# Widening the stretch of retention in which no adaLN sums are placed

## The chip, the cores and the metric

The kernel runs on one core of one Trainium2 chip. The metric is the device time of one execution in microseconds. Three executions of the kernel before are at hand, and one more that was profiled.

## What is computed

A decoder trunk of two layers over 256 tokens of 1024 features. Each layer is a half-step SwiGLU FFN, a mixer (retention in layer 0, a gated short convolution in layer 1) and a second half-step FFN. Every sub-layer works on an RMS norm that is scaled, shifted and gated by numbers which a conditioning vector gives (adaLN). Cut to what matters here:

```python
mod = (silu(c) @ ada_w[l] + ada_b[l])            # 9 x 1024 numbers a layer: shift, scale, gate of 3 sub-layers
h = rmsnorm(x, norm_g) * (1 + scale) + shift      # each sub-layer's input
x = x + gate * sublayer(h)                        # 0.5 * gate in the two FFNs

proj = h @ w_in                                   # retention: q, k, v of 4 heads, and g
o = rmsnorm((q k^T * decay) v, gn_g)              # per head, 256 queries, 512 value features
y = (silu(g) * o) @ w_out
```

## The kernel before

The 256 tokens lie along the free axis, features along the 128 partitions. Each float32 operand is split into a high and a low half in float32r, and a product is three products of halves (`product`, L278). A weight tile of 1 MB (128 x 2048) goes through the same stations every time: a DMA on SyncE's queue into one of five raw buffers (L235), a cast to the high half on ScalarE (`split_high`, L248, two pieces of 1024 columns), the low half by a subtraction on VectorE or, for every third tile's second piece, on GpSimd (L253), then TensorE. The list `jobs` (L200 to L223) holds all weight tiles in their order, and `weights()` (L268) hands out the next one and prepares the tiles up to four ahead. One gate tile or output tile of 1 MB takes TensorE about 5.6 us.

Retention (L634) runs its tiles in this order: three gate tiles, eight query and key tiles, eight value tiles (two for each of heads 0 to 3), the other five gate tiles, eight output tiles. From the first value tile on, a list of steps (L734 to L744) interleaves four things: the value projection of a head or a gate tile; `values` of the head before (L694: scores times values on TensorE, two copies out of PSUM on ScalarE at L705, four squares at L344, three additions of squares on GpSimd at L351); `normalize` of the head before that (L713: a sum over partitions on TensorE at L361, a square root on ScalarE at L373, a reciprocal on VectorE at L379, four multiplications at L717); and `apply` (L725: the normalized head times silu(g) at L729, split into halves `og` at L334 and L335). A gate tile leaves PSUM through a copy on ScalarE (L315) and an addition on VectorE (L316), and ScalarE then takes its silu in two halves (L321). Silu and square root need different tables on ScalarE, and a scheduler puts an ACT_TABLE_LOAD wherever the next function's table is not the one loaded. Of PSUM's four buffers one holds the conditioning vector by then, so the products turn over in three.

The conditioning product runs beside all that, off TensorE. `ada_load` (L109) fetches a 1 MB tile of `ada_w` into a raw buffer, and `ada_reduce` (L116) makes two sums of it on VectorE (one multiply-and-sum of 1024 columns and one read of the accumulator each, L120). 64 such tiles are placed among the weight tiles by `pace` (L187), which `weights()` calls for every tile n from the ninth on: it first makes the sums of tiles that were loaded, and then loads the next one if the count of loaded tiles is behind a straight line over the blocks of weights. It does neither around the first tile of an output product (`outputs`), nor for the first three tiles of a sub-layer (`begins`, `BIASED` = 3). Whatever a sub-layer still lacks is forced by `need` (L182), for the scale at the sixth output block and for the gate ahead of the outputs. A scheduler then orders each engine's instructions by readiness and priority; engines run what they hold in that order.

The next sub-layer's input is made as the output blocks are finished: `residual` (L510: L516, L518, L521 or L523), a square (L344), and `scaled` (L395), which makes h = x * scale in halves (L414 on ScalarE, L415 on VectorE) and therefore needs the scale. `whole` (L434) later makes the normalized input from the reciprocal r (L440, L441, L334, L335).

Of the kernel before, what the change touches and what calls it, by code (L numbers as in the profile page):

```python
# [31 lines left out]
BIASED = 3  # L32
# [3 lines left out]
BEFORE = 1  # L36
BEHIND = 1
# [29 lines left out]
def trunk_kernel(ctx: ExitStack, tc: tile.TileContext, a: dict, out: bass.AP):  # L67
# [97 lines left out]
    @within(behind)  # L165
    def reduce_loaded():
        while loaded:
            loaded.pop(0)()

    @within(behind)  # L170
    def run_side():
        kind, *args = side.pop(0)
        if kind == "ada":
            raw = ada_load(*args)
            loaded.append(lambda: ada_reduce(*args, raw))
            state["ada"] += 1
        elif kind == "table":
            nc.sync.dma_start(out=table, in_=a["table"])
        else:
            loaded.append(lambda: (ada_scale if kind == "scale" else ada_gate)(*args))  # L180
# [6 lines left out]
    def pace(n):  # L187

        state["spent"] += jobs[n][1] // P
        if any(o - BEFORE <= n < o + BEHIND for o in outputs) or any(b <= n < b + BIASED for b in begins):
            return
        reduce_loaded()
        if side and state["ada"] < n_ada * state["spent"] / (PACE * n_blocks):
            run_side()


    jobs = []  # L200
    outputs = []
    begins = []
    ready = {}
    for l in range(DEPTH):
        for f in range(2):
            if f == 1:
                begins.append(len(jobs))
                if l % 2 == 0:
                    jobs += [(a["ret_g"][j], 2048) for j in range(BIASED)]
                    jobs += [(a["ret_qk"][j], 2048) for j in range(8)]  # L210
                    jobs += [(a["ret_v"][h, i], 2048) for h in range(HEADS) for i in range(2)]
                    jobs += [(a["ret_g"][j], 2048) for j in range(BIASED, 8)]
                    outputs.append(len(jobs))
                    jobs += [(a["ret_out"][d], 2048) for d in range(KB)]
                else:
                    jobs += [(a["conv_cu"][d], 2048) for d in range(KB)]
                    jobs += [(a["conv_b"][j], 2048) for j in range(KB // 2)]
                    outputs.append(len(jobs))
                    jobs += [(a["conv_out"][j], 2048) for j in range(KB // 2)]
            begins.append(len(jobs))  # L220
            jobs += [(a["ffn_in"][l, f, b], 2048) for b in range(FB)]
            outputs.append(len(jobs))
            jobs += [(a["ffn_out"][l, f, d, i], 1408) for d, i in OUT_ORDER]  # L223
# [44 lines left out]
    def weights():  # L268
        n = state["next"]
        state["next"] += 1  # L270
        while state["loaded"] < min(n + AHEAD, len(jobs)):
            prepare_next()
        if n >= FIRST_GROUP:
            pace(n)
        return ready.pop(n)
# [618 lines left out]
```

## Time and profile before

| what | value |
|---|---|
| three executions | 1076.92, 1080.54 and 1081.19 us, median 1080.54 |
| the profiled execution | 1079.4 us |
| its span | 1077.6 us |
| TensorE, matmul busy | 1051.5 us, 98% of the span |
| VectorE, ScalarE, GpSimd busy | 845.5, 622.0 and 410.7 us |
| DMA | 268.39 MB, mean 249 GB/s |
| mean granted TensorE clock | 0.996 of full speed |

The span is what the profiler saw of the program on the core; 1.8 us of the execution's own time lie around it. Busy shares are means over stages; where an engine idles and what ended the idle time tells which of them sets the end.

### The profile page before, as it was taken

The numbers are of one execution on the slowest core, as the hardware profiler recorded it, in microseconds if no ns is written. First come the engines' busy times: TensorE is split into PE (matmuls) and PEld (weight loads), VectorE is DVE, ScalarE is ACT, GpSimd is POOL, SyncE is SP. The second block draws the span as 40 slices with busy tenths as digits, with TensorE's granted clock in tenths as the row PEclk, the third lists the DMA queues.
The fourth block names the chain that finished last, engine by engine and source line by source line (L and its number), as shares of the span: only waits on it lengthen the run. The fifth ranks groups of instructions, "written<-read, shape, count | busy, mean of one in ns | idle before, by whom it ended". The sixth has DMA issues, their size and how long they took to land.

```text
span 1077.6 us, 17508 instructions
## 1 busy us (share of the span) xinstructions
PE 1051.5 (98%) x6642; PEld 945.9 (88%) x6642; DVE 845.5 (78%) x1137; ACT 622.0 (58%) x1048; POOL 410.7 (38%) x357
## 2 busy tenths in 40 slices
PE   8999999999998999999999999999999989999996
PEld 6999988999886889888888988888898889888885
DVE  6899777899658898997777899777799888655444
ACT  4365545763366667566555766655576577655442
POOL 1034356254335432433345243335433433324352
PEclk9999999999999999999999999999999999999999
DMA  9977788868565576787679778777877544554441
GB/s 340 368 277 275 296 279 314 314 224 326 225 234 196 195 290 221 289 325 280 241 234 323 262 294 319 272 253 265 311 254 261 207 161 175 199 201 139 148 134 40
DMA packets 44566, 268.39 MB, mean 249 GB/s; under 512 B 4801, under 2 KB 6977, under 8 KB 19906
## 3 DMA queue, kind: packets, MB, share of 16 engines
q1 hardware_dynamic: 43138, 266.56, 68.1%
q8 instruction: 52, 0.85, 0.3%
q10 hardware_dynamic: 1344, 0.71, 0.2%
q14 instruction: 32, 0.26, 0.1%
HBM read 266.20 MB, written 1.05 MB: 248 GB/s over the span
## 4 chain that ended last, share of the span: by engine, by line
PE 57%; DVE 3%; issue 1%; ACT 0%; DVEq 0%; ACTq 0%
PE ps L288 33%; PE ps L292 19%; PE ps L291 2%; PE ps L290 2%; DVE lo L253 1%; DVE whole L335 0%; DVE rsum L518 0%; PE ps L361 0%; DVE h L415 0%; DVE raw L816 0%; ACT hi L248 0%; DVE xr L440 0%; DVE r L812 0%; DVE sum L328 0%; DVE av L594 0%
## 5 line engine op out<-in xcount | busy, mean ns | idle before, releaser
L253 DVE TENSOR_TENSOR lo<-raw,hi 128x1024 fp32r<-128x1024 f32 (+1 forms) x300 | 370.4, 1244 | 148.9 <-ACT hi L248 138.1
L248 ACT CAST hi<-raw 128x1024 fp32r<-128x1024 f32 (+2 forms) x408 | 377.0, 937 | 167.0 <-PE ps L288 65.5
L288 PE MATMUL ps<-whole,hi 128*128 128x512 f32 x1136 | 398.8, 396 | 2.4 <-ACT std L373 1.6
L292 PE MATMUL ps<-whole,lo 128*128 128x256 f32 x1264 | 353.8, 280 | 0.0
L253 POOL TENSOR_TENSOR lo<-raw,hi 128x384 fp32r<-128x384 f32 (+1 forms) x108 | 202.6, 1877 | 230.0 <-ACT hi L248 228.4
L288 PEld LDWEIGHTS ps<-whole,hi 128*128 128x128 f32 x1136 | 213.7, 188 | 53.3 <-ACT std L373 2.0
L292 PEld LDWEIGHTS ps<-whole,lo 128*128 128x128 f32 x1264 | 239.4, 189 | 0.1
L288 PE MATMUL ps<-act,hi 128*128 128x512 f32 x616 | 217.7, 398 | 0.6 <-DVE rsum L518 0.6
L292 PE MATMUL ps<-act,lo 128*128 128x256 f32 x704 | 197.8, 281 | 0.0
L335 POOL TENSOR_TENSOR act<-av,act 128x256 fp32r<-128x256 f32 x88 | 81.9, 933 | 202.4 <-ACT act L334 201.6
L120 DVE CUSTOM_DVE_ANT_0 raw<-raw,ps,misc 128x1024 f32<-128x1024 f32 x124 | 154.7, 1274 | 0.0
L288 PEld LDWEIGHTS ps<-act,hi 128*128 128x128 f32 x616 | 115.7, 188 | 29.7 <-DVE rsum L518 1.6
L292 PEld LDWEIGHTS ps<-act,lo 128*128 128x128 f32 x704 | 133.1, 189 | 0.3 <-DVE lo L253 0.3
L290 PE MATMUL ps<-h,hi 128*128 128x258 f32 (+1 forms) x464 | 131.8, 284 | 1.0 <-DVE sum L328 0.9
L291 PE MATMUL ps<-h,hi 128*128 128x258 f32 (+1 forms) x464 | 131.0, 282 | 1.5 <-DVE h L415 1.4
L292 PE MATMUL ps<-h,lo 128*128 128x258 f32 (+1 forms) x464 | 130.3, 281 | 0.0
L291 PEld LDWEIGHTS ps<-h,hi 128*128 128x128 f32 x464 | 87.9, 190 | 2.5 <-DVE h L415 2.4
L290 PEld LDWEIGHTS ps<-h,hi 128*128 128x128 f32 x464 | 87.6, 189 | 1.5 <-ACT sg L321 1.1
L292 PEld LDWEIGHTS ps<-h,lo 128*128 128x128 f32 x464 | 87.6, 189 | 0.0
L334 ACT CAST act<-av 128x256 fp32r<-128x256 f32 x88 | 35.3, 405 | 77.0 <-DVE av L592 70.5
L316 DVE TENSOR_TENSOR sum<-ps,sum 128x512 f32<-128x512 f32 x71 | 48.7, 685 | 19.7 <-ACT sum L315 19.7
L321 ACT ACTIVATE sg<-sum 128x256 f32<-128x256 f32 x79 | 32.6, 415 | 47.7 <-DVE sum L316 25.7
(135 smaller groups left out, 1425.4 us busy)
## 6 DMA issues: line engine op xcount, KB each, us to landing
raw<-in_ffn_in SPq DMA_DIRECT2D x80, 1024.0 KB, 4.9
raw<-in_ada_w SPq DMA_DIRECT2D x64, 1024.0 KB, 5.1
raw<-in_ffn_out SPq DMA_DIRECT2D x64, 704.0 KB, 5.1
raw<-in_ada_w SPq DMA_DIRECT2D x16, 512.0 KB, 7.2
raw<-in_ffn_in SPq DMA_DIRECT2D x16, 512.0 KB, 8.2
raw<-in_ret_g SPq DMA_DIRECT2D x8, 1024.0 KB, 4.9
raw<-in_ret_qk SPq DMA_DIRECT2D x8, 1024.0 KB, 5.3
raw<-in_ret_v SPq DMA_DIRECT2D x8, 1024.0 KB, 5.0
```

What stands on the lines that cost most here:

```text
L120: ins = nc.vector.tensor_tensor_reduce(out=w, in0=w, in1=state["cond"], scale=1.0, scalar=misc[:, C_ADAB + 72 * l + col:C_ADAB + 72 * l + ...
L248: nc.scalar.copy(out=hi, in_=raw[:, c:c + m])
L253: eng.tensor_tensor(out=lo, in0=raw, in1=hi, op=ALU.subtract)
L288: nc.tensor.matmul(out=ps, lhsT=hi, rhs=m.rearrange("p n s -> p (n s)"), start=start, stop=False)
L290: nc.tensor.matmul(out=ps, lhsT=hi, rhs=m[:, 0], start=start, stop=False)
L291: nc.tensor.matmul(out=ps, lhsT=hi, rhs=m[:, 1], start=False, stop=False)
L292: nc.tensor.matmul(out=ps[:, :n], lhsT=lo, rhs=m[:, 0], start=False, stop=stop)
L316: nc.vector.tensor_tensor(out=y[:, :, :S], in0=ps[:, :, :S], in1=y[:, :, :S], op=ALU.add)
L321: nc.scalar.activation(out=out, in_=y[:, i, :S], func=AF.Silu)
L334: hi = nc.scalar.copy(out=dst[:, 0], in_=src)
L335: lo = eng.tensor_tensor(out=dst[:, 1], in0=src, in1=dst[:, 0].bitcast(F32), op=ALU.subtract)
```

## The change

`pace` gets a length for every start in `begins`. The starts that were there keep three tiles. One more is added: from the last value tile on (`len(jobs) - 1` at that point of the list), six tiles, which are this value tile and the five gate tiles behind it. The last gate tile was already left out before, being next to the first output tile.

```diff
         state["spent"] += jobs[n][1] // P
-        if any(o - BEFORE <= n < o + BEHIND for o in outputs) or any(b <= n < b + BIASED for b in begins):
+        if any(o - BEFORE <= n < o + BEHIND for o in outputs) or any(b <= n < b + m for b, m in begins):
             return
@@
             if f == 1:
-                begins.append(len(jobs))
+                begins.append((len(jobs), BIASED))
                 if l % 2 == 0:
                     jobs += [(a["ret_g"][j], 2048) for j in range(BIASED)]
                     jobs += [(a["ret_qk"][j], 2048) for j in range(8)]
                     jobs += [(a["ret_v"][h, i], 2048) for h in range(HEADS) for i in range(2)]
+                    begins.append((len(jobs) - 1, 9 - BIASED))
                     jobs += [(a["ret_g"][j], 2048) for j in range(BIASED, 8)]
                     outputs.append(len(jobs))
@@
-            begins.append(len(jobs))
+            begins.append((len(jobs), BIASED))
             jobs += [(a["ffn_in"][l, f, b], 2048) for b in range(FB)]
```

The changed file has one blank line more above L193 and one line more in the list, so its lines below are numbered two higher (L323 there is L321 here). Since a scheduler orders the instructions, three places are shown in the built programs' order, before and after.

First, ScalarE from the copy of the first gate tile behind the values (`sum`) to the squares of head 3 (`sq<-o`), before:

```order
L315 COPY sum<-ps 128x2x256
L373 ACTIVATE std<-ps,eps 128x256
L334 CAST h_4447<-mod_95 128x2
L321 ACT_TABLE_LOAD
L321 ACTIVATE gate<-sum 128x256 x2
L705 COPY o<-ps 128x512 x2
L344 ACTIVATE sq<-o 128x256 x3
```

and with the change:

```order
L317 COPY sum<-ps 128x2x256
L323 ACT_TABLE_LOAD
L323 ACTIVATE gate<-sum 128x256
L375 ACT_TABLE_LOAD
L375 ACTIVATE std<-ps,eps 128x256
L323 ACT_TABLE_LOAD
L323 ACTIVATE gate<-sum 128x256
L707 COPY o<-ps 128x512 x2
L346 ACTIVATE sq<-o 128x256 x3
```

The square root `std` of head 2 now stands between the two silu halves, with a table load on either side of it, and the cast of a shift (`h<-mod`) is gone from here.

Second, VectorE at the same place, from the low half of a gate tile's weights on, before:

```order
L253 TENSOR_TENSOR lo<-raw,hi 128x1024
L120 ISA raw,mod_95<-raw,ps,misc 128x1024
L120 ISA mod_95 128x1
L120 ISA raw,mod_95<-raw,ps,misc 128x1024
L120 ISA mod_95 128x1
L316 TENSOR_TENSOR sum<-ps,sum 128x2x256
L379 RECIPROCAL r<-std 128x256
L717 SCALAR_TENSOR_TENSOR o<-o,misc,r 128x256 x4
L729 TENSOR_TENSOR o<-o,gate 128x256 x2
```

and with the change:

```order
L255 TENSOR_TENSOR lo<-raw,hi 128x1024
L318 TENSOR_TENSOR sum<-ps,sum 128x2x256
L731 TENSOR_TENSOR o<-o,gate 128x256
L381 RECIPROCAL r<-std 128x256
L731 TENSOR_TENSOR o<-o,gate 128x256
L719 SCALAR_TENSOR_TENSOR o<-o,misc,r 128x256 x4
```

The two sums of an adaLN tile (L120) are gone, and the two products of head 1 with the gate tile moved to both sides of the reciprocal.

Third, VectorE at the entry of the FFN behind retention, from the last output block's residual (`x_94<-ps`) to the reciprocal r of the new norm, before:

```order
L523 SCALAR_TENSOR_TENSOR x_94<-ps,gt_104,x_94 128x256
L351 TENSOR_TENSOR acc<-acc,sq 128x256
L415 SCALAR_TENSOR_TENSOR h_4519<-x_94,sc_99,h_4519 128x256
L253 TENSOR_TENSOR lo<-raw,hi 128x1024
L379 RECIPROCAL r<-std 128x256
```

and with the change:

```order
L525 SCALAR_TENSOR_TENSOR x_94<-ps,gt_104,x_94 128x256
L255 TENSOR_TENSOR lo<-raw,hi 128x1024
L353 TENSOR_TENSOR acc<-acc,sq 128x256
L417 SCALAR_TENSOR_TENSOR h_4514<-x_94,sc_99,h_4514 128x256
L120 ISA raw,mod_95<-raw,ps,misc 128x1024
L120 ISA mod_95 128x1
L120 ISA raw,mod_95<-raw,ps,misc 128x1024
L120 ISA mod_95 128x1
L255 TENSOR_TENSOR lo<-raw,hi 128x1024
L381 RECIPROCAL r<-std 128x256
```

One adaLN tile's sums now stand between the last half of h and the reciprocal. TensorE's own order is the same in both programs.

## Rows read from the trace of the kernel before

**Rows 1.** The profile page: the span, the engines' busy time with share and instruction count.

```profile
span 1077.6 us, 17508 instructions
PE 1051.5 (98%) x6642; PEld 945.9 (88%) x6642; DVE 845.5 (78%) x1137; ACT 622.0 (58%) x1048; POOL 410.7 (38%) x357
```

**Rows 2.** What TensorE waited for over the whole span: the waiting line and what released it, us in total, times, the longest.

```profile
PE ps L361 <- POOL acc L351: 3.4, 1, 3.4
...
PE ps L288 <- ACT std L373: 1.6, 1, 1.6
PE ps L291 <- DVE h L415: 1.4, 2, 0.8
...
PE ps L288 <- DVE whole L335: 0.8, 1, 0.8
```

**Rows 3.** TensorE in order of time around its longest wait: start, us, instruction, and in brackets the idle time before it with what released it.

```profile
338.42 0.50 PE L288 MATMUL ps<-whole,hi 128*128 128x512 f32 x1 [1.60 <-ACT std L373]
...
344.06 0.28 PE L292 MATMUL ps<-whole,lo 128*128 128x256 f32 x1
347.70 0.70 PE L361 MATMUL ps<-acc,ones 128*128 128x256 f32 x2 [3.36 <-POOL acc L351]
```

**Rows 4.** The stretch right behind that wait and the next one: us, busy time of each engine, the granted TensorE clock as a share of full speed, DMA share, GB/s.

```profile
348.70:352.10 3.40, 3.40 (x12) 2.87 (x11) 3.14 (x4) 1.68 (x3) 0.62 (x1) 0.50 0.01 2
352.10:365.00 12.90, 12.90 (x76) 11.27 (x75) 9.77 (x15) 9.54 (x15) 4.30 (x5) 1.00 0.52 186
```

**Rows 5.** ScalarE in order of time from the gate tile's copy to the table load for head 3's square root.

```profile
337.42 0.58 ACT L315 COPY sum<-ps 128x512 f32<-128x512 f32 x1
337.89 0.47 ACT L373 ACTIVATE std<-ps,eps 128x256 f32<-128x256 f32 x1
340.29 0.20 ACT L334 CAST h<-mod 128x2 fp32r<-128x2 f32 x1 [1.92 <-DVE mod L120]
340.50 1.28 ACT L321 ACT_TABLE_LOAD   x1
341.80 0.72 ACT L321 ACTIVATE gate<-sum 128x256 f32<-128x256 f32 x2
342.43 1.05 ACT L705 COPY o<-ps 128x512 f32<-128x512 f32 x2
343.37 1.04 ACT L344 ACTIVATE sq<-o 128x256 f32<-128x256 f32 x3
...
346.13 1.04 ACT L248 CAST hi<-raw 128x1024 fp32r<-128x1024 f32 x1
347.19 1.28 ACT L373 ACT_TABLE_LOAD   x1
```

**Rows 6.** VectorE in order of time at the same place.

```profile
337.78 1.27 DVE L120 CUSTOM_DVE_ANT_0 raw<-raw,ps,misc 128x1024 f32<-128x1024 f32 x1
...
340.18 0.68 DVE L316 TENSOR_TENSOR sum<-ps,sum 128x512 f32<-128x512 f32 x1
340.78 1.73 DVE L379 RECIPROCAL r<-std 128x256 f32<-128x256 f32 x1
342.55 1.68 DVE L717 SCALAR_TENSOR_TENSOR o<-o,misc,r 128x256 f32<-128x256 f32 x4
```

**Rows 7.** GpSimd in order of time at the same place.

```profile
344.29 0.10 POOL L378 MEMSET r<- 128x2 f32 x1 [3.54 <-DVE o L717]
344.38 1.10 POOL L351 TENSOR_TENSOR acc<-sq 128x256 f32<-128x256 f32 x1
345.56 0.72 POOL L351 TENSOR_TENSOR acc<-acc,sq 128x256 f32<-128x256 f32 x1
346.24 0.73 POOL L335 TENSOR_TENSOR og<-o,og 128x256 fp32r<-128x256 f32 x1
346.92 0.72 POOL L351 TENSOR_TENSOR acc<-acc,sq 128x256 f32<-128x256 f32 x1
347.60 1.72 POOL L335 TENSOR_TENSOR og<-o,og 128x256 fp32r<-128x256 f32 x1
```

**Rows 8.** VectorE, and one instruction of GpSimd, in order of time at the entry of the FFN behind retention.

```profile
411.52 0.41 DVE L351 TENSOR_TENSOR acc<-acc,sq 128x256 f32<-128x256 f32 x1
...
413.83 2.39 POOL L253 TENSOR_TENSOR lo<-raw,hi 128x1024 fp32r<-128x1024 f32 x1 [6.72 <-ACT hi L248]
414.10 2.40 DVE L351 TENSOR_TENSOR acc<-acc,sq 128x256 f32<-128x256 f32 x1 [1.38 <-ACT sq L344]
416.43 0.47 DVE L415 SCALAR_TENSOR_TENSOR h<-x,sc,h 128x256 fp32r<-128x256 f32 x1
418.45 1.23 DVE L253 TENSOR_TENSOR lo<-raw,hi 128x1024 fp32r<-128x1024 f32 x1 [1.56 <-ACT hi L248]
419.60 1.75 DVE L379 RECIPROCAL r<-std 128x256 f32<-128x256 f32 x1
```

**Rows 9.** TensorE's two waits in that FFN's first tiles, in order of time.

```profile
416.95 0.39 PE L291 MATMUL ps<-h,hi 128*128 128x258 f32 x1 [0.59 <-DVE h L415]
...
434.79 0.50 PE L288 MATMUL ps<-whole,hi 128*128 128x512 f32 x1 [0.80 <-DVE whole L335]
```

**Rows 10.** Two tiles of that FFN with an adaLN tile beside each: columns as in rows 4 (TensorE, its weight loads, VectorE, ScalarE, GpSimd).

```profile
446.80:452.40 5.60, 5.60 (x34) 4.85 (x33) 5.60 (x7) 3.04 (x6) 4.58 (x3) 1.00 1.00 383
452.40:458.00 5.60, 5.60 (x34) 4.86 (x33) 5.60 (x9) 3.29 (x6) 1.11 (x3) 1.00 1.01 405
```

## The prediction

> **What bounds the kernel now.** I read the profile page first: TensorE's matmuls are busy for 1051.5 of 1077.6 us [rows 1], so no engine beside it can give more than TensorE's own idle time, some 26 us in the whole program. The list of what TensorE waited for comes next. Its longest single wait is 3.4 us for an addition on GpSimd, and the next one inside the program's body is 1.6 us for a square root on ScalarE [rows 2]. TensorE in order of time puts both into the stretch that the change touches: the gate tile that starts at 338.42 came 1.60 us late, and behind it the sum of head 3's squares at 347.70 came 3.36 us late [rows 3]. The reader is to see a third loss there: right behind the long wait the granted clock is 0.50, TensorE's 1.2 GHz, for 3.40 us, and 1.00, or 2.4 GHz, afterwards [rows 4]. At half the rate 3.40 us do 1.70 us of work, so the fall cost 1.70 us. Together 1.60 + 3.36 + 1.70 = 6.66 us hang on this place, and that is the most that can be won here.
>
> Why was it late? Follow ScalarE and VectorE through it. VectorE was free of the tile's low half at 337.78, made two sums of an adaLN tile (1.20 us from start to start and a second one like it), and came to the gate tile's addition only at 340.18 [rows 6]. ScalarE waited 1.92 us for the second of these sums with the cast of a shift, loaded the silu table at 340.50, ran two silu halves, and only at 342.43 copied head 3 out of PSUM; the squares began at 343.37 [rows 5]. GpSimd added them from 344.38 to 347.64, with a product for `og` between the additions [rows 7], and TensorE went on at 347.70. So an adaLN tile did stand in the chain. The question is what stands there when it is gone.
>
> **Step 1: head 3's squares.** Removed: two sums, 340.18 - 337.78 = 2.40 us on VectorE, and ScalarE's wait for them. The gate tile's copy starts at 337.42 for 0.58 us as before, as nothing ahead of it moves, so ScalarE is free at 338.00, and not at 340.50: 2.50 us earlier. Added, as the order shows: the silu table, one silu half, the square root's table, the square root of head 2, the silu table again, the other half. A table load is 1.28 us, with 0.02 us to its activation (340.50 to 341.80), a silu half 0.36 us (half of 0.72), the root 0.47 us [rows 5]. From 338.00: load until 339.28, half until 339.66, load until 340.96, root until 341.45, load until 342.75, half until 343.13. Head 3's copies then start at about 343.10 in place of 342.43. The root was free before, since it ran inside the 1.92 us wait; now it and two more loads are in the path: 2 x 1.30 + 0.47 + 0.10 = 3.17 us put in for 2.50 us taken out, a net delay of 0.67 us.
>
> GpSimd gives most of this back. Before, its first addition had to wait for a memset that waited for VectorE until 344.29, although the second square was done at about 344.10, and took 1.10 us where the others take 0.72 [rows 7]. With the change that memset comes after two additions. The second square ends at 344.10 + 0.67 = 344.77; additions until 345.55 and 346.27, the memset 0.10, `og` 0.73, the last addition 0.72: 347.82, against 347.64 before. The memset needs the four multiplications of head 2: root until 341.45, reciprocal 1.73 (343.18), one gate product about 0.40, multiplications 1.68, so 345.3; that is in time. **Step 1: +0.18 us.** Lower end: had the two added loads cost nothing, -2.60 + 0.18 = -2.4 us. Upper end: the first addition at 1.10 again (+0.38) and the `og` at 1.72, as the next one took [rows 7] (+0.99): +1.6 us. I take +0.18, from the durations met most often.
>
> TensorE's wait ahead of it changes its name, not its worth. The gate tile took its PSUM buffer behind head 2's root; now it takes the one that the former gate tile's addition frees, which can run at 338.05 (copy done) for 0.68 us, so TensorE starts at about 338.75, not 338.42 [rows 3, 5, 6]. These 0.33 us lie in front of a wait that ends by GpSimd anyway: 0.
>
> **Step 2: the clock.** TensorE would still idle from 338.75 + 5.92 (338.42 to 344.34, when it went idle) = 344.67 to 347.85, 3.2 us against 3.36. The nearest row is the wait of 3.36 us, after which the clock fell [rows 3, 4]; I take the fall as unchanged, 0. Ends: -1.70 without it, +1.70 with a second one elsewhere.
>
> **Step 3: the second adaLN tile of the stretch.** It leaves VectorE between the fifth and the seventh gate tile. TensorE waited for nothing there, and ran at full clock [rows 4]: 0.
>
> **Step 4: where the tiles go.** Two tiles are owed. They follow one per weight tile in the output blocks, so the scale of the next sub-layer comes later, and the h halves of blocks 0 to 3 are made in one group. The count of sums ahead of the last h is the same. But one tile's two sums now stand between that h and the reciprocal r. Before, VectorE idled 1.56 us there for a cast [rows 8]. Of 2.40 us, 1.56 are hidden and 0.85 us are not: r at 420.45, not 419.60. All of `whole` hangs on r, VectorE has no gap behind it, and TensorE waited 0.80 us for its seventh part [rows 9]; that wait becomes 1.65. **Step 4: +0.85 us.** Lower end: the last h comes earlier, since its addition took 2.40 us beside a GpSimd subtraction [rows 8] where the one at 411.52 took 0.41; then TensorE's 0.59 us at 416.95 [rows 9] go, and less of the 0.85 is left: -0.6. Upper end: nothing is hidden, +2.4.
>
> **Step 5: the catching up.** Up to eight FFN tiles in a row then carry an adaLN tile, where there were five. Such a tile already fills VectorE (5.60 of 5.60 us) and the DMA engines (share 1.00), yet TensorE stays busy for all of it [rows 10]. What lags by a tile or two is caught by PSUM's three buffers and the weights prepared four tiles ahead: 0. Upper end: one lost overlap like the 2.00 us too long addition of rows 8, +2.0.
>
> **The sum** is +0.18 + 0.85 = +1.0 us on the profiled execution's 1079.4: 1080.4 us. The median of the runs shown is 1.1 us higher, 1080.54, and would give 1081.5; I forecast between the two, **1080.9 us**, no change that can be told from none. About 0.5% (5.4 us) is what a measurement of this kernel can resolve.
>
> The Trainium skill speaks against this change: "ScalarE: Activation LUTs", section "What ACT_TABLE_LOAD costs", puts a drain of some 1.38 us on top of each load, 2.66 us in all. The row does not agree: a cast that began at 346.13 for 1.04 us is followed by a load at 347.19, 0.02 us after it ended [rows 5]. By the page's figure step 1 would cost 2.8 us more, an estimate.
>
> **The rivals.**
>
> *A, the intended gain (0.06).* The chain ends as much earlier as the sums were long: the wait of 3.36 us shrinks by 2.4, and the clock does not fall: -2.4 - 1.7 = -4.1, with step 4 at its lower end -4.7: 1074.7 us. For it: the sums stood in the chain [rows 5, 6]. Against it: two table loads take their place, and every load in these rows takes 1.28 us. Only the whole 6.66 us would pass 0.5%.
>
> *B, a slower one (0.07), at the FFN's entry.* VectorE's two sums ahead of r fall on the same time as a GpSimd subtraction, and r and `whole` pay for both: 2.40 for the sums, 2.0 for an operation held up as at 414.10 [rows 8], and TensorE's wait of then 0.80 + 4.4 = 5.2 us is followed by a fall of the clock as behind the 3.36 us one, 1.70: +6.1 plus step 1, 1085.7 us. It decides from the point where r is more than about 2.5 us late, at 422. Against it: VectorE's idle 1.56 us are there to be filled.
>
> *C, the loads cost double (0.03).* If each switch also emptied the engine for about as long again, step 1 would be 2 x 1.3 = 2.6 us worse: 1083.5 us. The skill's figure above would make it so; the row at 347.19 stands against it.
>
> *D, it does not do what it says.* Only one of the two tiles that leave stood in head 3's chain, and the tile whose sums run ahead of head 1's root stays, being loaded before the last value tile. That is part of the forecast.
>
> **The numbers.** The forecast's case has 0.84: its own ends are 1076.0 (runs as scattered as before, 1076.92 the lowest, with the clock's fall gone) and 1085.5 (1081.19, the highest, with steps 1 and 4 at their upper ends, 1.4 + 1.6 more, and some of step 5). This already reaches C, and A and B lie just outside: range 1076.0 to 1085.5. Faster by over 0.5% needs the most of A: 0.03. Slower by over 0.5% is B with a little of step 5: 0.05. Within: 0.92.
>
> **What would show it.** ScalarE's rows would show three table loads between the gate tile's copy and head 3's copies, and these copies about 5.7 us behind the copy's start (343.10 - 337.42; 5.01 before). TensorE's longest wait would still be for the addition on GpSimd, at 3.0 to 3.7 us, with one stretch at a granted clock of 0.50 behind it; its wait at the gate tile would name VectorE. At the FFN's entry an L120 pair would stand ahead of the reciprocal, and the wait for `whole` would be about 1.6 us. The prediction is wrong if the long wait falls below 1.5 us, if the low clock is gone or comes twice, or if TensorE idles in the eight FFN tiles.

## The result, and the profile after

The changed kernel takes 1082.26 us (median of 20 runs, 1078.63 to 1085.48), the kernel before 1079.94 us (20 runs, 1076.2 to 1083.27): a ratio of 1.0020 with a 95% interval of 1.0011 to 1.0029, so 1.2 to 3.1 us slower, 2.2 in the middle. That is less than the 0.5% named as the limit, but with 20 runs of each kernel it can be told from none, and it is about a microsecond more than the sum in the prediction. The profiled execution took 1081.45 us. Of the runs further below, one execution of copies_first_b, 1144.89 us, was in a slower state of the chip and counts in no ratio and no mean clock.

The page of the changed kernel, for [rows 1]: a longer span, with all engines' work the same to within 3 us.

```profile
span 1079.7 us, 17502 instructions
PE 1054.0 (98%) x6642; PEld 948.2 (88%) x6642; DVE 846.2 (78%) x1137; ACT 624.4 (58%) x1050; POOL 413.2 (38%) x357
```

TensorE in order of time, for [rows 2, 3, 9], and the stretches of low clock with one of full clock, for [rows 4] (columns as there).

```profile
339.55 0.50 PE L290 MATMUL ps<-whole,hi 128*128 128x512 f32 x1 [2.02 <-DVE sum L318]
...
348.85 0.70 PE L363 MATMUL ps<-acc,ones 128*128 128x256 f32 x2 [1.90 <-POOL acc L353]
...
417.81 0.36 PE L293 MATMUL ps<-h,hi 128*128 128x258 f32 x1 [1.88 <-DVE h L417]
...
436.33 0.50 PE L290 MATMUL ps<-whole,hi 128*128 128x512 f32 x1
```

```profile
340.16:343.56 3.40, 3.40 (x13) 2.81 (x12) 1.92 (x2) 3.34 (x5) 0.63 (x1) 0.50 0.52 149
348.85:352.25 3.40, 3.40 (x19) 3.00 (x20) 3.18 (x3) 2.63 (x5) 1.62 (x1) 1.00 0.01 2
418.68:422.08 3.40, 3.40 (x16) 3.25 (x16) 3.40 (x6) 3.23 (x4) 0.00 (x0) 0.50 0.85 328
```

Three things moved. The wait for the gate tile grew from 1.60 to 2.02 us. The low clock came 8.5 us earlier, inside that tile: TensorE worked more slowly on a tile behind which it had to wait anyway, so the wait for head 3's squares reads 1.90 instead of 3.36, and the stretch behind it runs at full clock. From the gate tile's first matmul to the sum of squares it is 348.85 - 339.55 = 9.30 us, and 9.28 before [rows 3]. And the FFN's entry has a wait of 1.88 us for h where there was one of 0.59, with a second stretch of low clock behind it. The matmul that waited 0.80 us for `whole` before, the one at 436.33 here, waits no more; but it stands 18.52 us behind the one that waited for h, where it stood 434.79 - 416.95 = 17.84 behind it [rows 9].

ScalarE and GpSimd at head 3, for [rows 5, 7], from the gate tile's copy on.

```profile
338.13 0.57 ACT L317 COPY sum<-ps 128x512 f32<-128x512 f32 x1
338.72 1.28 ACT L323 ACT_TABLE_LOAD   x1
340.01 0.42 ACT L323 ACTIVATE gate<-sum 128x256 f32<-128x256 f32 x1
340.45 1.28 ACT L375 ACT_TABLE_LOAD   x1
341.74 0.47 ACT L375 ACTIVATE std<-ps,eps 128x256 f32<-128x256 f32 x1
342.23 1.28 ACT L323 ACT_TABLE_LOAD   x1
343.53 0.42 ACT L323 ACTIVATE gate<-sum 128x256 f32<-128x256 f32 x1
343.85 1.06 ACT L707 COPY o<-ps 128x512 f32<-128x512 f32 x2
...
345.67 0.91 POOL L353 TENSOR_TENSOR acc<-sq 128x256 f32<-128x256 f32 x1 [4.88 <-ACT sq L346]
346.66 0.73 POOL L353 TENSOR_TENSOR acc<-acc,sq 128x256 f32<-128x256 f32 x1
...
348.07 0.72 POOL L353 TENSOR_TENSOR acc<-acc,sq 128x256 f32<-128x256 f32 x1
```

The three table loads stand there. Head 3's copies start 343.85 - 338.13 = 5.72 us behind the gate tile's copy (5.01 before), and the last addition ends 348.79 - 338.13 = 10.66 us behind it (347.64 - 337.42 = 10.22 before): 0.44 us late.

VectorE at the FFN's entry with one instruction of GpSimd, for [rows 8].

```profile
405.50 1.27 DVE L120 CUSTOM_DVE_ANT_0 raw<-raw,ps,misc 128x1024 f32<-128x1024 f32 x1
...
406.70 1.27 DVE L120 CUSTOM_DVE_ANT_0 raw<-raw,ps,misc 128x1024 f32<-128x1024 f32 x1
...
412.09 1.21 DVE L255 TENSOR_TENSOR lo<-raw,hi 128x1024 fp32r<-128x1024 f32 x1
413.62 1.20 DVE L255 TENSOR_TENSOR lo<-raw,hi 128x1024 fp32r<-128x1024 f32 x1
413.75 3.64 POOL L255 TENSOR_TENSOR lo<-raw,hi 128x1024 fp32r<-128x1024 f32 x1 [6.78 <-ACT hi L250]
414.76 0.41 DVE L353 TENSOR_TENSOR acc<-acc,sq 128x256 f32<-128x256 f32 x1
415.09 2.58 DVE L417 SCALAR_TENSOR_TENSOR h<-x,sc,h 128x256 fp32r<-128x256 f32 x1
...
421.13 1.74 DVE L381 RECIPROCAL r<-std 128x256 f32<-128x256 f32 x1
```

Two adaLN tiles' sums now follow each other (403.96 to 409.10), since the owed tiles came late and `need`, called at the sixth output block, also makes the sums of the tile just loaded. They push two low halves of weights to 412.09 and 413.62, onto the start of GpSimd's subtraction, which takes 3.64 us in place of 2.39. The addition that took 2.40 us before takes 0.41, but h itself takes 2.58 in place of 0.47 and ends when the subtraction does.

### The profile page after: what moved, and what is told of

Same layout as the page of the kernel before. It is cut to its first block, busy times and chain, and to the rows that moved or that the text cites. A ratio compares the mean times of both kernels' runs of the same rounds, so it can differ in the third digit from the quotient of the medians.

```text
span 1079.7 us, 17502 instructions
## 1 busy us (share of the span) xinstructions
PE 1054.0 (98%) x6642; PEld 948.2 (88%) x6642; DVE 846.2 (78%) x1137; ACT 624.4 (58%) x1050; POOL 413.2 (38%) x357
## 4 chain that ended last, share of the span: by engine, by line
PE 59%; DVE 2%; issue 0%; ACT 0%; DVEq 0%; ACTq 0%
PE ps L290 33%; PE ps L294 20%; PE ps L293 3%; PE ps L292 3%; DVE lo L255 1%; DVE h L417 0%; PE ps L363 0%; DVE rsum L520 0%; DVE raw L818 0%; DVE r L814 0%; DVE x L523 0%; ACT hi L250 0%; DVEq L891 0%; DVE x L525 0%; ACT std L375 0%
## 5 line engine op out<-in xcount | busy, mean ns | idle before, releaser
L120 DVE CUSTOM_DVE_ANT_0 raw<-raw,ps,misc 128x1024 f32<-128x1024 f32 x124 | 154.5, 1272 | 0.0
L323 ACT ACTIVATE sg<-sum 128x256 f32<-128x256 f32 x79 | 32.6, 415 | 49.4 <-DVE sum L318 27.4
```

The source lines that it names most:

```text
L120: ins = nc.vector.tensor_tensor_reduce(out=w, in0=w, in1=state["cond"], scale=1.0, scalar=misc[:, C_ADAB + 72 * l + col:C_ADAB + 72 * l + ...
L323: nc.scalar.activation(out=out, in_=y[:, i, :S], func=AF.Silu)
```

## The experiments

The theory drawn from the two traces before any of these runs: the change gains about 1.1 us at head 3 (TensorE's start there, seen from its work ahead, moved by +0.44 us, and 1.56 us of low clock fell into a wait) and loses 2.0 us at the FFN's entry, by h and the low clock behind it. Its rivals: the prediction's own steps (table loads at head 3, sums ahead of r), and a loss at head 3 alone. The numbers of the theories in the quoted expectations begin anew with each run.

All times are medians; ratios are to the kernel before, run on the same chip. "Clock" is the mean granted clock over the runs; the kernel before has 0.9948 (35 runs), the change 0.9943.

| run | us | ratio, 95% interval | clock |
|---|---|---|---|
| sums_one_later | 1083.07 | 1.0021, 1.0010 to 1.0033 | 0.9941 |
| entry_clear | 1082.95 | 1.0016, 1.0004 to 1.0027 | 0.9942 |
| root_first | 1079.13 | 0.9984, 0.9973 to 0.9994 | 0.9959 |
| copies_first | 1078.12 | 0.9972, 0.9959 to 0.9986 | 0.9958 |
| copies_first_b | 1076.52 | 0.9966, 0.9954 to 0.9978 | 0.9957 |
| entry_fixed | 1078.38 | 0.9993, 0.9979 to 1.0006 | 0.9948 |
| lo_vector | 1085.00 | 1.0040, 1.0024 to 1.0056 | 0.9934 |
| both_b | 1075.60 | 0.9964, 0.9950 to 0.9977 | 0.9964 |
| both | 1074.15 | 0.9951, 0.9932 to 0.9969 | 0.9963 |
| before_again, after_again | 1077.38, 1080.12 | one execution each | 0.998, 0.995 |

### Head 3 alone: sums_one_later

The kernel before, `begins` with lengths as in the change, and one start of its own:

```diff
+                    begins.append((len(jobs), 1))
                     jobs += [(a["ret_g"][j], 2048) for j in range(BIASED, 8)]
```

> The kernel before, with one thing changed: the first gate tile behind the values makes no sums, so the two sums of ada(0,2,6) come one tile later; every load and the FFN's entry stay as before. Theory 1 (the two traces: the change gained at head 3 and lost more at the FFN's entry): ScalarE has the change's three table loads here too, TensorE waits 2.0 us at the gate tile and 1.9 us at the sum of head 3's squares instead of 1.6 and 3.4, the granted clock is 0.50 once, inside that gate tile, and the run is 1.1 us faster than before (0.999). Theory 2 (the prediction's steps): a wait of 3.2 us, the low clock behind it, +0.2 us. Theory 3 (the change's loss sits at head 3, in the table loads): 1 to 2.6 us slower.

Measured: 1.0021, 2.3 us slower than before. Theory 1 fell. ScalarE's order and the waits at head 3 are those of the change, and so is the low clock inside the gate tile; but a second stretch of it follows the second wait, and a new wait of 1.41 us for a product of the gate appears ahead of the outputs, with nothing edited but the place of the sums:

```profile
339.35 0.71 PE L289 MATMUL ps<-whole,hi 128*128 128x512 f32 x1 [2.02 <-DVE sum L317]
348.64 0.70 PE L362 MATMUL ps<-acc,ones 128*128 128x256 f32 x2 [1.90 <-POOL acc L352]
...
378.65 0.50 PE L289 MATMUL ps<-og,hi 128*128 128x512 f32 x1 [1.41 <-POOL og L336]
```

So the gain read at head 3 was no gain of the change's order: here the waits are the same, and the clock falls a second time behind them. The time would suit theory 3 as well, but 1.41 us of it are the wait ahead of the outputs, which the change does not have, so this run sets no price on the table loads.

### The table loads: root_first

The projection of a gate tile now returns its silu as a function (`run_`), which is called behind head 2's square root (`roots[0]`) and ahead of head 3's copies and squares (`next(vals)`, behind the second silu half, `roots[1]`):

```diff
-            run()
+            run_ = run()
...
+                blocks, acc = raw_o[step - 2]
+                std = rms([acc], DV)
...
+                    with tc.issue_after(roots[0]):
+                        run_()
+                    with tc.issue_after(roots[1]):
+                        raw_o[step - 1] = next(vals)
```

> The change, with head 2's square root ordered ahead of both silu halves of the first gate tile on ScalarE, and head 3's copies behind them as in the change: two table loads less there, and nothing else moved on ScalarE. Theory 1: head 3's copies start 2.6 us earlier (3.1 us behind the gate tile's copy's start instead of 5.7), the wait for the addition on GpSimd goes from 1.9 to under 0.3 us, 1.6 to 1.9 us faster than the change. Theory 2 (the prediction: GpSimd gives most of a shift of the copies back, its memset waits for VectorE): the wait moves by less than 1 us. If a load costs 2.66 us in place of 1.3, the copies start 5.3 us earlier.

Measured: 0.9984, by the ratios 3.9 us less than the change. ScalarE and TensorE:

```profile
339.21 0.58 ACT L317 COPY sum<-ps 128x512 f32<-128x512 f32 x1
339.69 0.48 ACT L375 ACTIVATE std<-ps,eps 128x256 f32<-128x256 f32 x1
340.19 1.28 ACT L323 ACT_TABLE_LOAD   x1
341.48 0.73 ACT L323 ACTIVATE gate<-sum 128x256 f32<-128x256 f32 x2
342.11 1.05 ACT L714 COPY o<-ps 128x512 f32<-128x512 f32 x2
...
347.27 0.70 PE L363 MATMUL ps<-acc,ones 128*128 128x256 f32 x2 [0.82 <-POOL acc L353]
```

The copies come 2.90 us behind the gate tile's copy instead of 5.72: two loads are worth 2.82 us with the gaps around them. The Trainium skill, "ScalarE: Activation LUTs", section "What ACT_TABLE_LOAD costs", would make it 5.3, an estimate; the rows do not agree. The wait falls to 0.82 us at full clock, against 3.37 at full clock in entry_fixed below, which has the change's order here: 2.55 us of 2.82 reached TensorE. GpSimd gives back little, so theory 2 fell. Theory 1 had the shift right (2.6 us), but the wait is not quite gone, and its 1.6 to 1.9 us in time were too few, since it took the wait as 1.90, shortened by the low clock ahead of it. The difference of the ratios is known to some 1.5 us either way; the mean granted clock, 0.9959 against 0.9943, can be another 1.7 us at most, and less where the low clock lay ahead of a wait.

### The silu out of the way: copies_first and copies_first_b

As root_first, but the copies stay ahead of the silu; in copies_first on the change, in copies_first_b on the kernel before, with the sums left in place:

```diff
+                    with tc.issue_after(roots[0]):
+                        run_()
```

> The change, with the first gate tile's silu put behind the copies and squares of head 3 and behind head 2's square root on ScalarE; no other engine's order moves but for these steps. Theory 1 (the table loads ahead of head 3's copies are what still holds TensorE at the sum of squares): head 3's copies start within 2 us of the gate tile's copy instead of 5.7, the wait for the addition on GpSimd (1.9 us) is gone, the wait of 2.0 us at the gate tile and the low clock behind it stay: 1.9 us faster than the change, 0.4 above before. Theory 2 (GpSimd's additions and products set the wait, whatever ScalarE does): the wait stays above 1 us and the time is that of the change. Theory 3 (the later silu makes the gate product and og late): a new wait at the outputs, slower than the change.

> The kernel before, with the adaLN sums left where they were, and on ScalarE the first gate tile's silu put behind head 3's copies and squares and head 2's square root (the edit of copies_first without the change). Theory 1 (what held TensorE at head 3 was the silu and its table load ahead of the copies, not the sums): the wait of 3.4 us for the addition on GpSimd is gone with the sums in place, the low clock behind it with it, the FFN's entry is the unchanged one with waits of 0.6 and 0.8 us: 3.4 to 5 us faster than before, 1075.8 to 1077.4, and level with copies_first or up to 1.3 us faster. Theory 2 (the sums do hold head 3): ScalarE or VectorE comes late by the sums' 2.4 us, a wait of 1 us or more stays, and the run is 1 us or more slower than copies_first.

Measured: 0.9972 and 0.9966. In copies_first_b the wait for the squares is gone with the sums still there:

```profile
339.82 0.50 PE L288 MATMUL ps<-whole,hi 128*128 128x512 f32 x1 [2.09 <-ACT std L373]
...
347.11 0.59 PE L361 MATMUL ps<-acc,ones 128*128 128x256 f32 x2
```

and head 3's copies start 0.48 us behind the gate tile's copy, at 338.33:

```profile
338.81 0.59 ACT L711 COPY o<-ps 128x512 f32<-128x512 f32 x1
...
341.20 0.19 ACT L334 CAST h<-mod 128x2 fp32r<-128x2 f32 x1
```

The cast that waited for the sums in [rows 5], and the silu whose input VectorE adds behind them [rows 6], now stand behind the copies. So the sums held TensorE only through ScalarE's order, which put the cast, the table load and the silu ahead of the copies; with the copies first, TensorE no longer waits at the squares. Which of the cast and the silu held more was not taken apart. By the ratios copies_first is 5.2 us faster than the change, where theory 1 said 1.9: in part the wait that went was longer than 1.90 at full clock, and the rest is open. copies_first_b is 3.7 us faster than before, within its theory 1. copies_first keeps a wait of 1.88 us for h at the entry, copies_first_b the old one of 0.59.

### The entry: entry_clear, entry_fixed, lo_vector

entry_clear takes the sums between h and r away; lo_vector leaves them, and puts GpSimd's subtraction on VectorE; entry_fixed does both. The first line is in entry_clear and entry_fixed, the second (tile 72 is the FFN's third) in lo_vector and entry_fixed:

```diff
                     outputs.append(len(jobs))
+                    begins.append((len(jobs) + 6, 2))
...
-            split_low(*split_high(*tile_), nc.gpsimd if last and (width % SPLIT or n % 3 == 0) else nc.vector)
+            split_low(*split_high(*tile_), nc.gpsimd if last and (width % SPLIT or n % 3 == 0 and n != 72) else nc.vector)
```

> The change, and nothing placed at the last two output tiles of retention: the two sums between the last h and the reciprocal r are gone from there, what is ahead of h stays. Theory 1 (the entry's loss is the wait for h and the low clock behind it, which the sums do not touch): TensorE still waits 1.9 us for h, the clock still falls once there, r comes 2.4 us earlier for nothing, and the time stays that of the change, 2.3 us above before, within 0.5. Theory 2 (the prediction's step 4: the sums ahead of r cost 0.85 us): 0.85 us faster than the change. Theory 3 (all of the entry's 2 us hangs on r): 2 us faster than the change, level with before.

> The kernel entry_clear (the change, nothing placed at the last two output tiles), and the low half that GpSimd makes beside the last h (the third FFN tile) made on VectorE. Theory 1 (the last h is late because it runs beside that subtraction): h takes 0.5 us in place of 2.6, TensorE's wait for it falls from 1.9 to under 0.3 us, no low clock there, the wait for whole stays at or under 1 us: 2 to 3 us faster than entry_clear, 1080 to 1081. Theory 2 (whole takes over): r and whole come no earlier, TensorE waits there for 2 us more than the 0.7, and the time is that of entry_clear within 0.5 us.

> The change, and the third FFN tile's low half made on VectorE in place of GpSimd, with the two adaLN sums still between the last h and the reciprocal r (entry_fixed without its other edit). Theory 1 (h and r each set the entry, whichever is later): the wait for h falls from 1.9 to about 1 us or less, but r starts no earlier than in the change, and the wait for whole grows from nothing to 2 to 3 us: half of entry_fixed's 2.9 us gain or less, 0 to 1.4 us faster than the change. Theory 2 (only h counts): as fast as entry_fixed, 2.9 us faster than the change, wait for whole under 1 us.

entry_clear, 1.0016, is level with the change, as its theory 1 said, though the runs cannot tell that from theory 2's 0.85 us: h still takes 2.57 us beside a subtraction of 3.63, and TensorE waits 1.88 us for it, then 0.74 for `whole`. Its r is not where it is in the change:

```profile
417.05 2.57 DVE L418 SCALAR_TENSOR_TENSOR h<-x,sc,h 128x256 fp32r<-128x256 f32 x1
...
422.38 1.75 DVE L382 RECIPROCAL r<-std 128x256 f32<-128x256 f32 x1
```

r starts 422.38 - 417.05 = 5.33 us behind the start of h, and 421.13 - 415.09 = 6.04 in the change, so the two sums ahead of r cost r 0.71 us there. entry_fixed, 0.9993, is 2.9 us faster than the change: h takes 0.48 and no wait for it is left. Its rows, TensorE and VectorE in order of time, and the clock behind the long wait:

```profile
350.27 1.22 PE L364 MATMUL ps<-acc,ones 128*128 128x256 f32 x2 [3.37 <-POOL acc L354]
...
418.38 0.48 DVE L418 SCALAR_TENSOR_TENSOR h<-x,sc,h 128x256 fp32r<-128x256 f32 x1
...
437.38 0.50 PE L291 MATMUL ps<-whole,hi 128*128 128x512 f32 x1 [0.70 <-DVE whole L338]
```

```profile
349.90:353.30 3.40, 3.03 (x9) 2.56 (x10) 2.66 (x2) 2.87 (x4) 1.99 (x2) 0.50 0.01 2
```

lo_vector came out worse than either theory said: 1.0040, by the ratios 5.1 us above entry_fixed, from which, on VectorE from the last h to r, only the two sums tell it apart. Here r starts at 422.33, and the last parts of `whole` come late one after another, with a longer stretch of low clock behind them:

```profile
436.01 0.50 PE L290 MATMUL ps<-whole,hi 128*128 128x512 f32 x1 [0.74 <-DVE whole L337]
438.87 0.80 PE L290 MATMUL ps<-whole,hi 128*128 128x512 f32 x1 [1.91 <-DVE whole L337]
```

```profile
438.05:444.80 6.75, 5.93 (x18) 5.06 (x19) 5.62 (x5) 2.78 (x4) 3.69 (x4) 0.50 0.55 167
```

So there are two chains into this FFN, h and r, and the change makes both late: h by the subtraction beside it, and r by h's delay and 0.71 us of sums. lo_vector takes h's delay away, but puts the subtraction's 1.21 us on VectorE ahead of r beside the sums, and that cost more than was won.

### Both repairs: both_b and both

> The kernel copies_first_b, and the third FFN tile's low half on VectorE in place of GpSimd: a version meant to beat both. If the entry's wait for h of 0.6 us goes and the wait for whole does not grow: 0.6 us faster than copies_first_b. If the 1.2 us of added work on VectorE reach r: the wait for whole grows by up to 1.2 us and it is up to 0.6 us slower than copies_first_b.

> The change with both repairs: the silu behind head 3's copies (as in copies_first) and the entry as in entry_fixed. Against both_b, which has the same repairs and leaves the sums where the kernel before has them. If moving the sums is worth something once neither place holds TensorE: 1 us or more faster than both_b (0.9964 of before). If it is worth nothing: level with both_b, 0.996 to 0.997.

Measured: 0.9964 and 0.9951, both faster than the kernel before and the change. both_b cannot be told from copies_first_b (0.9966), so neither of its two expectations is settled. The intervals of both_b and both overlap, so whether moving the sums is worth anything once nothing else holds TensorE stays open: 1.4 us by the points, none by the bounds. The two profiles show no wait that moving them took away: 2.09 and 2.02 us at the gate tile, none above 0.25 us at head 3's sum or for h, and 0.70 and 0.69 for `whole`.

### Two executions of one program: before_again and after_again

> The kernel before, unchanged, profiled once more, to see what two executions of the same program differ in. If waits are set by the program: 1.6 and 3.4 us at head 3 and 0.6 and 0.8 at the FFN's entry again, within 0.1. The low clock: 3.4 us at 0.50 behind the long wait again, if a wait of that length is always followed by it; somewhere else, or not at all, if it is not. The pace of the weight tiles: 35.3 or 34.7 us for 200 matmuls in the FFN from 461 to 532 us in both executions alike, if the program sets it.

> The change, unchanged, profiled once more. If its waits are set by the program: 2.0 us at the gate tile and 1.9 for h again; at head 3's sum 1.9 us if the granted clock is 0.50 inside the gate tile ahead of it, and 3.5 us if it is not; a wait for whole of about 1.5 us if no low clock lies between h and whole, none if it does.

before_again waited 1.61, 3.37, 0.59 and 0.81 us at the four places, as [rows 3, 9] did, but no low clock followed the long wait, and the FFN behind ran at another pace. The two rows, then the stretch behind the long wait and the FFN, before_again:

```profile
348.27 0.70 PE L361 MATMUL ps<-acc,ones 128*128 128x256 f32 x2 [3.37 <-POOL acc L351]
...
415.95 0.38 PE L291 MATMUL ps<-h,hi 128*128 128x258 f32 x1 [0.59 <-DVE h L415]
```

```profile
348.30:352.30 4.00, 4.00 (x23) 3.52 (x24) 3.74 (x3) 3.27 (x5) 1.60 (x1) 1.00 0.01 2
440.00:530.00 90.00, 90.00 (x522) 78.67 (x521) 82.27 (x107) 53.09 (x91) 32.88 (x30) 1.00 0.81 304
```

and the same FFN in the profile of before that the prediction read:

```profile
440.00:530.00 90.00, 90.00 (x512) 78.07 (x511) 82.26 (x106) 53.07 (x91) 31.73 (x30) 1.00 0.81 302
```

after_again had the waits of the change at head 3, with the low clock inside the gate tile again. At the entry it had both waits, and no low clock there:

```profile
418.67 0.36 PE L293 MATMUL ps<-h,hi 128*128 128x258 f32 x1 [1.30 <-DVE h L417]
...
437.16 0.50 PE L290 MATMUL ps<-whole,hi 128*128 128x512 f32 x1 [1.39 <-DVE whole L337]
```

Here the waits are 1.30 + 1.39 = 2.69 us, against 0.59 + 0.80 = 1.39 before. They do not hold the whole cost, because TensorE itself came later to the first of them. TensorE's order is the same in both kernels, so one can time it between the same two matmuls: from one of the output product to the one that waits for h. The first of these, in the profile of before, in the change's and in after_again:

```profile
370.15 0.27 PE L292 MATMUL ps<-og,lo 128*128 128x256 f32 x1
...
369.72 0.27 PE L294 MATMUL ps<-og,lo 128*128 128x256 f32 x1
...
370.48 0.28 PE L294 MATMUL ps<-og,lo 128*128 128x256 f32 x1
```

To h it is 46.80 us before, 48.09 in the change and 48.19 in after_again. Without the waits that is 46.21, 46.21 and 46.89: TensorE took 0.68 us more in after_again, at full clock, and its wait for h was 0.58 shorter. From h to the matmul that waits for `whole` it is 17.84 before, 18.52 in the change and 18.49 in after_again. So the entry costs 1.97 us (66.61 against 64.64) in one execution and 2.04 in the other, and against the first theory the low clock in the first of them cost nothing on top.

The low clock behind the long wait did cost something. From the sum of squares to the matmul that waits for h it is 416.95 - 347.70 = 69.25 us before, and 415.95 - 348.27 = 67.68 in before_again: 1.57 us, where half of 3.40 was counted.

## Why the prediction was right, and where its steps were not

The time lies in the range, 1082.26 us against a forecast of 1080.9, and slower rather than faster held. "No change that can be told from none" held for a limit of 0.5%, but not for 20 runs, which tell 1.2 to 3.1 us from none; the sum of +1.0 lies just under that. Its reason held at head 3: the sums went out of the chain and two table loads went in. But most of the loss is at the FFN's entry, where one of two terms was put at nothing. That the time still lies in the range is owed more to the range's 9.5 us than to the sum. The steps:

- **Step 1** (+0.18): right in mechanism, too small. The copies were to be 5.7 us behind the gate tile's copy and were 5.72. But GpSimd gave back 0.27 of the 0.71 us, not 0.49: the first addition took 0.99 us to the next one's start, where 0.78 were counted. The sum was 0.44 us late. The wait at the gate tile names VectorE, as said, at 2.02 us. By root_first the two loads are what the stretch paid.
- **Step 2** (0, the clock): wrong by the prediction's own list, since the low clock came twice in the profile. It had rested on one execution of one wait, and before_again shows the same 3.37 us wait with no low clock behind it. Its cost was taken as 1.70 us and measured 1.57. A wait of 2.0 us at the gate tile was followed by it in 7 of the 11 profiles that have this wait, and not in the other 4. In both profiles of the change each fall lay ahead of a wait that covered it. Over the runs the mean granted clock went from 0.9948 to 0.9943, which is 0.5 us of 1080 at most.
- **The long wait** was to stay at 3.0 to 3.7 us and reads 1.90. It was not shortened: where the gate tile ran at full clock, in entry_fixed, it is 3.37.
- **Step 3** (0): TensorE waited for nothing there in the change. That the place is not free is shown by the 1.41 us of sums_one_later.
- **Step 4** (+0.85): the step that failed, by its size. The place was right and so was the term for r: the sums ahead of it cost 0.71 us by entry_clear. The term for h was put at nothing, with an earlier h as the lower end. The count of sums ahead of the last h was the same, as said, but they came in a row, and this the step did not follow up: it expected h earlier, because an addition had been held up beside GpSimd's subtraction [rows 8], and h took that place. That the sums in a row brought h there is read from the rows; no run spreads them. The wait for h went from 0.59 to 1.88, that for `whole` from 0.80 to 1.39 where no low clock hid it (1.65 was said), and r came 1.96 us late by the same matmuls (421.13 - 369.72 against 419.60 - 370.15), not 0.85. The entry costs 2.0 us more.
- **Step 5** (0): right. TensorE was busy for 90.00 of 90.00 us from 440 to 530, in both.

With the low clock kept apart the terms measure 0.44 + 1.97 = 2.4 us where 1.0 were summed, and the runs say 1.2 to 3.1. Executions of the kernel before in which the clock falls behind the long wait, as in one of its two profiles, are 1.57 us slower by it, and the change is that much less behind them; how many executions do so is open. Of the rivals, A's 6.66 us were not all to be won: copies_first_b won 3.7 of them without moving the sums, and the wait at the gate tile stayed in every edited kernel, at 2.02 or 2.09 us. B's chain is what lo_vector shows, r past 422 and the low clock behind the waits; in the change itself it was h that ran beside GpSimd's subtraction, and r came later by that and by the sums. C falls with root_first.

## What to carry to other kernels

Before work is moved out of a chain, look at what a scheduler will put into the gap: here the two halves of an activation closed round a square root, and two table loads, 2.82 us, cost more than the 2.40 us of sums had. An order that keeps functions of one table together, and a chain's copies ahead of work that nobody waits for yet, was worth 3.7 us with nothing moved. Work that is owed lands somewhere: follow not only how much of it stands ahead of the next critical step, but whether it comes in one piece.

## What the runs showed of the hardware

- Two executions of one program ran the FFN from 440 to 530 us at two paces: 512 matmuls and 522 in the same 90 us, with TensorE busy throughout and the granted clock at 1.00 in both (511 and 521 in the two of the change). The output product shows it too, 46.21 us and 46.89. Over such a stage that is 1.7 us, as much as the whole effect studied here; what sets the pace is open. Differences of 2 us between two single profiles are no evidence until they are tied to a wait.
- VectorE and GpSimd held each other up by whole instructions. VectorE's low half at 413.62 ended at 414.82 and its addition at 415.17; GpSimd's subtraction, begun at 413.75, ended 2.39 us (its length before) after 415.00, and h ended 0.28 us after it. The Trainium skill, "SBUF — State Buffer", section "Who interferes with whom", says that an operation of VectorE with two inputs in SBUF contends with one of GpSimd that reads SBUF, and that the lock on the ports that they share is exclusive; the rows agree.
- A stretch at half clock cost 1.57 us where nothing followed that could cover it, and nothing where it lay ahead of a wait that another engine ended: the wait behind the gate tile went from 3.37 to 1.90 us, with 9.28 us between the same matmuls at full clock and 9.30 with the low clock; at the entry these were 18.49 without it and 18.52 with it.
